# Order of the split products in a half tile of weights: high half first, low half last

## The chip, the cores and the metric

The kernel runs on one core of a Trainium2 chip. The metric is the device time of one execution in microseconds. It is a whole program: weights and activations come from HBM, and the outputs go back to it.

## What is computed

Two passes of one transformer-like layer share their weights: a context pass over 128 tokens and a denoising pass over 128 tokens, each with 2048 features. In short:

```
mod  = silu(c) @ w_ada + b_ada             # six vectors: shift, scale and gate, twice
h    = rmsnorm(x) * (1 + scale1) + shift1
p    = h @ w_in                            # 2048 -> 8192 features
mix  = [gated linear recurrence, short convolution, attention](p)
x    = x + gate1 * (mix @ w_out)           # 2048 -> 2048
h    = rmsnorm(x) * (1 + scale2) + shift2
x    = x + gate2 * ((silu(h @ wg) * (h @ wu)) @ wd)   # hidden width 5632
out  = rmsnorm(x)
```

All of it is in fp32. The weights are read once for both passes, which is nearly all of the 330 MB that the kernel reads.

## The kernel before, in words

**Products in two halves.** [...] To keep the precision, both operands of a large product are split into a high half and the rest: `hi` is the number rounded, `lo` the difference. A product x*w is then the sum of three: x.hi*w.hi, x.lo*w.hi and x.hi*w.lo. The activations lie split already (`lhs[:, s, 0]` and `lhs[:, s, 1]`, `s` being the sample: 0 context, 1 denoising). The weights are split as they come.

**A tile of weights.** A tile is 512 rows by 512 columns, 1 MB, in SBUF as 128 partitions x 4 blocks `k` x 512. `split` (line 238) issues its DMA on SyncE's queue (line 243) into one of four `raw` buffers and splits it in two half tiles of two blocks each: ScalarE copies `hi` from `raw` (line 253), VectorE subtracts to get `lo` (line 254). There are three buffers of each (`HL_BUFS`). For the first two rounds of the input projection the tiles are only half as large, one half tile each.

**The products.** `split_mm` (line 265) goes over the blocks of a tile and over the two samples; for each, `products` (line 258) issues three matmuls of 128x128 by 128x512 into the sample's accumulator `acc[s]` (one accumulator of 512 columns for each sample, two such pairs in all). The order in the source is x.hi*w.hi, x.lo*w.hi, x.hi*w.lo for sample 0, the same for sample 1, and then the next block: twelve matmuls for a half tile, of which eight read `hi` and four `lo`. `last_mm` (line 273) does the last two tiles of an output block in another way: it splits them into buffers of their own, and then runs all products of sample 0 before those of sample 1. `feature_mm` (line 285) is a third form, for narrow tiles with the weights as the stationary operand; its products are at line 304.

**What runs beside it.** The layer's modulation vectors are also products with large weights, `w_ada`. A part of them is done on TensorE between the tiles (`ada_pe`, line 328), on `raw` tiles that are not split. The rest is done on VectorE: `later_dve` (line 397) loads rows of `w_ada` into two buffers `araw` (a small copy on GpSimd at line 407, then a DMA from GpSimd's queue at line 408) and accumulates them with four instructions a piece (line 411). After each tile `behind` (line 442) issues as much of that as the constants `PACE_T` and `PACE_V` allow for the stage.

**The order of the instructions.** The source gives the order only in part. The program is built under a framework (`TileContext` with `schedule_with_timeline_sim=True`, line 1112) that knows what each instruction reads and writes, takes the source's order as a priority and places each engine's instructions by when a model of the chip has their operands ready. `split` stands in a scope of higher priority, in the later stages by 600 (`SPLIT_AHEAD`), so that loads and splits go ahead of other work. Each engine then runs its queue strictly in that order. A `hi` buffer is written again when the last matmul that reads it has ended, and so with `lo`; a `raw` buffer is loaded again when both halves have been made from it.

**The stages.** 0 to 240 us: modulation of the first norm and seven column blocks of the input projection in rounds over the rows; to 525 us: the other column blocks, with recurrence, convolution and attention in between; to 626 us: the output projection; then the second norm and the channel mixer, in two groups of hidden columns.

Of the kernel before, what the change touches and what calls it, by code (L numbers as in the profile page):

```python
# [92 lines left out]
def trunk(ctx: ExitStack, tc: tile.TileContext, a: dict):  # L93
    nc = tc.nc
# [12 lines left out]
    def u4(shape=(P, 2, CH)):  # L107
        return sb(list(shape), "u4", U4_BUFS)

    def u8(shape=(P, 2, 2, 4, P), dt=F32):  # L110
        return sb(list(shape), "u8", U8_BUFS, dt)

    def st(shape=(P, CH), dt=F32):
        return sb(list(shape), "st", ST_BUFS, dt)
# [5 lines left out]
    def accs():  # L120
        r = []
        for s in range(2):
            uid[0] += 1
            r.append(psum.tile([P, CH], F32, tag="acc", name=f"acc_{uid[0]}", bufs=4))
        return r
# [112 lines left out]
    def split(src, apart=False):  # L238

        n = src.shape[1]  # L240
        with tc.high_priority(offset=ahead[0]):
            raw = sb([P, 4, CH], "raw", RAW_BUFS)
            nc.sync.dma_start(raw[:, 0:n], src)
            parts = []
            if apart:
                his, los = u8((P, 4, CH), F32R), u8((P, 4, CH), F32R)
            for j in range(n // 2):
                if apart:
                    hi, lo = his[:, 2 * j:2 * j + 2], los[:, 2 * j:2 * j + 2]
                else:  # L250
                    hi = sb([P, 2, CH], "hi", HL_BUFS, F32R)
                    lo = sb([P, 2, CH], "lo", HL_BUFS, F32R)
                nc.scalar.activation(hi, raw[:, 2 * j:2 * j + 2], AF.Copy)  # L253
                nc.vector.tensor_tensor(lo, raw[:, 2 * j:2 * j + 2], hi.bitcast(F32), op=ALU.subtract)  # L254
                parts.append((hi, lo))
        return parts

    def products(acc, s, k, lhs, lk, parts, first, last):

        hi, lo = parts[k // 2]  # L260
        for i, (x, w) in enumerate(((0, hi), (1, hi), (0, lo))):
            nc.tensor.matmul(acc, lhsT=lhs[:, s, x, lk, :], rhs=w[:, k % 2, :],  # L262
                             start=first and i == 0, stop=last and i == 2)

    def split_mm(src, acc, lhs, first, last, k0=0):

        parts = split(src)
        n = src.shape[1]
        for k in range(n):
            for s in range(2):  # L270
                products(acc[s], s, k, lhs, k0 + k, parts, first and k == 0, last and k == n - 1)

    def last_mm(steps, acc, phase):

        tiles = []
        for src, lhs in steps:
            tiles.append((split(src, True), lhs))
            behind(phase)
        for s in range(2):
            for t, (parts, lhs) in enumerate(tiles):  # L280
                for k in range(4):
                    products(acc[s], s, k, lhs, k, parts, False, t == len(tiles) - 1 and k == 3)
            yield s

    def feature_mm(src, rhs, accs2, first, last):
# [156 lines left out]
    def behind(phase=None):  # L442

        pump()
        if phase is not None:
            ada_step(phase)
# [45 lines left out]
    for nm in ("xp", "xs"):  # L492
        t = u8((P, D))
# [370 lines left out]
    for ri, (k0, nk) in enumerate(ROUNDS):  # L864
        nxt = 4 * ROUNDS[ri + 1][1] // 2 if ri + 1 < len(ROUNDS) else 0
        last = ri == len(ROUNDS) - 1
        if last:
            ahead[0] = SPLIT_AHEAD
        for i, name in enumerate(ORDER[:START]):
            acc = accs()  # L870
            split_mm(w_in(k0 // 4, name)[:, k0 % 4:k0 % 4 + nk, :], acc, hT[k0 // 4], True, True, k0 % 4)
            if ri == 0:
                part[name] = u4()
            for s in range(2):
                if ri == 0:
                    nc.scalar.activation(part[name][:, s, :], acc[s], AF.Copy)
                else:
                    nc.vector.tensor_tensor(part[name][:, s, :], part[name][:, s, :], acc[s], op=ALU.add)  # L878
            behind(0 if last else None)
            if ri == 0 and i == 1:  # L880
                spawn(other_inputs(part[name][:, 0, :]))
            if i < START - 1:
                first_step((nxt * (i + 1)) // (START - 1) - (nxt * i) // (START - 1))
            if last:
                consume(name, part[name])
    for name in ORDER[START:]:
        if name in FM:
            for half in range(2):
                acc = accs()
                for q in range(2):  # L890
                    feature_mm(a["w_infm"][2 * FM.index(name) + half, q],
                               lambda k: tuple(hT[2 * q + k // 4][:, :, x, k % 4, :] for x in range(2)), acc, q == 0, q == 1)
                    behind(1)
                for b in range(2):
                    consume_fm(name, 2 * half + b, acc[b][:, 0:256].rearrange("p (s t) -> p s t", s=2))
            continue
        acc = accs()
        for q in range(4):
            split_mm(w_in(q, name), acc, hT[q], q == 0, q == 3)
            behind(1)  # L900
        t = u4()
        for s in range(2):
            nc.scalar.activation(t[:, s, :], acc[s], AF.Copy)
        consume(name, t)
# [4 lines left out]
    for n in range(4):  # L909
        acc = accs()  # L910
        xr = sb([P, 2, CH], "ld", 2)
        nc.gpsimd.tensor_copy(xr[:, :, 0:1], S["late"][:, :, 0:1])
        for s, nm in enumerate(("xp", "xs")):
            nc.gpsimd.dma_start(xr[:, s, :], a[nm][:, n * CH:(n + 1) * CH])
        if n == 3:
            for p in range(GAP_APART):
                gap[p] = [u4(), u4()]
                for j in range(2):
                    nc.sync.dma_start(gap[p][j], a["w_ada2"][LATER_GAP - 8, p, :, 2 * j:2 * j + 2])

        def add(s):
            t = st()
            nc.vector.tensor_tensor(t, acc[s], g[:, s, :], op=ALU.mult)
            nc.vector.tensor_tensor(x[:, s, :], t, xr[:, s, :], op=ALU.add)
            nc.scalar.activation(t, x[:, s, :], AF.Square, accum_out=ssq2[:, s, n:n + 1])

        many = 4 - LAST_TILES if n == 3 else 4
        for j in range(many):
            split_mm(a["w_out"][n, j], acc, mix[j], j == 0, j == 3)
            behind(2)  # L930
        x = u4()
        x1.append(x)
        g = gate(8 + n)
        for s in last_mm([(a["w_out"][n, j], mix[j]) for j in range(many, 4)], acc, 2):
            add(s)
        if n == 2:
            rest2 = [most(ssq2[:, s, 0:3]) for s in range(2)]
# [57 lines left out]
    for gi, grp in enumerate(groups):  # L995
# [6 lines left out]
        for n in range(4):  # L1002
            acc = accs()
# [7 lines left out]
            for s in last_mm([(a["w_down"][n, grp[j]], fs[j]) for j in range(many, len(grp))], acc, 3):  # L1011
                t = st()
                v = x1[n][:, s, :]
                nc.vector.tensor_tensor(t, acc[s], g[:, s, :], op=ALU.mult)
                nc.vector.tensor_tensor(v, v, t, op=ALU.add)
                if gi == 0:
                    continue
                nc.scalar.activation(t, v, AF.Square, accum_out=ssq3[:, s, n:n + 1])
                if not final:
                    nc.vector.tensor_tensor(v, v, fw[:, n, :], op=ALU.mult)  # L1020
                    if n == 2:
                        rest3.append(most(ssq3[:, s, 0:3]))
                    continue

                r = rms1(ssq3[:, s, 3:4], D, rest3[s])
                out = a["o_ys" if s else "o_yp"]
                for b in (2, 0, 3, 1):
                    v = x1[b][:, s, :]
                    if b == 3:
                        nc.vector.scalar_tensor_tensor(v, v, r, fw[:, 3, :], op0=ALU.mult, op1=ALU.mult)  # L1030
                    elif b == 2:
                        nc.vector.tensor_scalar(v, v, r, None, op0=ALU.mult)
                    else:
                        nc.scalar.activation(v, v, AF.Copy, scale=r)
                    (nc.scalar if b < 2 else nc.sync).dma_start(out[:, b * CH:(b + 1) * CH], v)
# [81 lines left out]
```

## Time and profile before

| | |
|---|---|
| runs | 1393.62 us median of 3 (1393.14 to 1399.99) |
| the profiled execution's own time | 1394.64 us |
| its span, from the first to the last instruction | 1392.8 us |
| mean granted TensorE clock | 0.991 |
| TensorE matmuls, weight loads | 1353.3 us (97%), 1082.0 us (78%) |
| VectorE | 875.9 us (63%) |
| ScalarE | 626.6 us (45%) |
| GpSimd | 135.3 us (10%) |
| matmuls | 7936 |
| HBM read | 330.43 MB, 240 GB/s over the span |

Matmuls overlap one another, so a matmul's own duration (some 0.39 us) is longer than the distance to the next one, and the busy share of TensorE says only that it had a matmul in flight. The distance between starts is its pace. In rows of the trace "L262" is a line of the kernel above, "acc<-hi,u" a matmul that writes `acc` and reads `hi` and a tile of the activations, "x2" two such instructions merged into one row; the time ahead of it is the start of the first, then their joint length. A bracket at the end gives how long the engine was idle before, and what ended that.

### The profile page before, as it was taken

How to read it: one execution, taken by the hardware profiler on the slowest of the kernel's cores; microseconds unless marked ns; L12 is line 12 of the kernel's file. 1: busy time of each engine (PE TensorE's matmuls, PEld its weight loads, DVE VectorE, ACT ScalarE, POOL GpSimd, SP SyncE). 2: the span in 40 equal slices, each digit the busy share in tenths (PEclk: the TensorE clock that was granted, in tenths of full speed). 3: DMA queues.
4: the chain of work that ended last, by engine and by line, in shares of the span. 5: the costliest groups of instructions: out<-in, count | busy, mean ns of one | idle time of the engine just before them, and what ended most of it. 6: DMA issues, size and time to landing. Idle time of an engine off the chain costs nothing.

```text
span 1392.8 us, 19779 instructions
## 1 busy us (share of the span) xinstructions
PE 1353.3 (97%) x7936; PEld 1082.0 (78%) x7936; DVE 875.9 (63%) x1102; ACT 626.6 (45%) x839; POOL 135.3 (10%) x201
## 2 busy tenths in 40 slices
PE   5999999999999999999899999999999999999996
PEld 3666777897798886677788788888888888888885
DVE  3354558987977886467745879545555544455565
ACT  4433347655455443346444344443334344444442
POOL 0100002221222321001200231000000000000000
PEclk9999999999999999999999999999999999999998
DMA  9797887775887988775665667555556555555551
GB/s 345 281 345 276 318 314 271 290 280 206 300 290 263 319 330 319 274 272 190 243 216 182 224 229 273 196 192 185 194 198 215 194 196 181 188 197 190 183 204 67
DMA packets 54380, 335.39 MB, mean 241 GB/s; under 512 B 7248, under 2 KB 7312, under 8 KB 19216
## 3 DMA queue, kind: packets, MB, share of 16 engines
q1 hardware_dynamic: 42768, 296.79, 58.7%
q0 software_dynamic: 10944, 36.29, 7.3%
q8 instruction: 62, 1.02, 0.3%
q10 hardware_dynamic: 576, 1.05, 0.2%
q14 instruction: 30, 0.25, 0.0%
HBM read 330.43 MB, written 3.67 MB: 240 GB/s over the span
## 4 chain that ended last, share of the span: by engine, by line
PE 89%; DMA 5%; issue 3%; DVE 2%; POOL 1%; ACT 1%; SPq 0%; DVEq 0%; POOLq 0%; ACTq 0%
PE acc L262 69%; PE acc L304 10%; PE ada L328 6%; DMA araw<-w_ada 2%; DMA raw<-w_ada 1%; PE aux L452 1%; DMA raw<-w_in 1%; DVE lo L254 1%; POOL araw L407 1%; DMA u<-xp 1%; PE aux L626 0%; PE aux L375 0%; DMA aacc<-b_ada 0%; DVE aacc L411 0%; PE aux L341 0%
## 5 line engine op out<-in xcount | busy, mean ns | idle before, releaser
L262 PE MATMUL acc<-hi,u 128*128 128x512 f32 x2944 | 873.4, 393 | 1.0 <-ACT u L484 0.8
L254 DVE TENSOR_TENSOR lo<-raw,hi 128x1024 fp32r<-128x1024 f32 x368 | 449.2, 1223 | 376.2 <-ACT hi L253 362.3
L262 PEld LDWEIGHTS acc<-hi,u 128*128 128x128 f32 x2944 | 551.6, 189 | 136.8 <-issue 11.2
L253 ACT ACTIVATE hi<-raw 128x1024 fp32r<-128x1024 f32 x368 | 388.7, 1060 | 556.1 <-PE acc L262 471.8
L262 PE MATMUL acc<-lo,u 128*128 128x512 f32 x1472 | 533.1, 394 | 7.1 <-DVE lo L254 7.1
L262 PEld LDWEIGHTS acc<-lo,u 128*128 128x128 f32 x1472 | 274.5, 188 | 77.5 <-DVE lo L254 11.6
L411 DVE SCALAR_TENSOR_TENSOR aacc<-araw,cs,aacc 128x512 f32<-128x512 f32 x224 | 159.4, 746 | 40.7 <-DMA araw<-w_ada 31.1
L304 PE MATMUL acc<-u,hi 128*128 128x256 f32 x768 | 141.8, 286 | 0.0
L304 PEld LDWEIGHTS acc<-u,hi 128*128 128x128 f32 x768 | 119.0, 191 | 7.3 <-issue 5.9
L304 PE MATMUL acc<-u,lo 128*128 128x256 f32 x384 | 108.1, 286 | 0.0
L328 PE MATMUL ada<-raw,cst 128*32 128x256 f32 (+1 forms) x784 | 92.3, 481 | 11.8 <-DMA raw<-w_ada 11.8
L407 POOL COPY araw<-u 128x2 f32<-128x2 f32 x56 | 54.0, 965 | 264.4 <-DVE aacc L411 212.7
L294 ACT ACTIVATE hi<-raw 128x1024 fp32r<-128x1024 f32 x48 | 50.9, 1060 | 64.0 <-PE acc L304 44.0
L304 PEld LDWEIGHTS acc<-u,lo 128*128 128x128 f32 x384 | 72.5, 191 | 5.2 <-issue 2.5
L295 DVE TENSOR_TENSOR lo<-raw,hi 128x1024 fp32r<-128x1024 f32 x48 | 58.4, 1221 | 15.3 <-ACT hi L294 12.5
L328 PEld LDWEIGHTS ada<-raw,cst 128*32 128x32 f32 x784 | 26.4, 113 | 44.3 <-issue 32.1
L878 DVE TENSOR_TENSOR u<-u,acc 128x512 f32<-128x512 f32 x56 | 37.7, 684 | 26.7 <-PE acc L262 26.7
L408 POOL DMA_DIRECT2D araw<-w_ada x56 | 30.0, 536 | 15.5 <-POOL araw L407 15.2
L401 POOL COPY aacc<-u 128x2 f32<-128x2 f32 x7 | 3.8, 536 | 252.3 <-DVE u L878 173.4
L480 ACT ACTIVATE st<-aux,sh,sc 128x128 f32<-128x128 f32 x48 | 18.1, 456 | 14.3 <-DVE sc L349 7.4
L262 PE MATMUL acc<-u,u 128*128 128x512 f32 x96 | 22.1, 389 | 0.0
L262 PEld LDWEIGHTS acc<-u,u 128*128 128x128 f32 x96 | 18.0, 188 | 3.7
(218 smaller groups left out, 631.8 us busy)
## 6 DMA issues: line engine op xcount, KB each, us to landing
raw<-w_ada SPq DMA_DIRECT2D x66, 1024.0 KB, 6.9
raw<-w_gate SPq DMA_DIRECT2D x44, 1024.0 KB, 4.9
raw<-w_up SPq DMA_DIRECT2D x44, 1024.0 KB, 4.8
raw<-w_down SPq DMA_DIRECT2D x44, 1024.0 KB, 4.8
raw<-w_in SPq DMA_DIRECT2D x33, 1024.0 KB, 6.5
araw<-w_ada POOLq DMA_DIRECT2D x56, 512.0 KB, 5.7
raw<-w_infm SPq DMA_DIRECT2D x24, 1024.0 KB, 6.2
raw<-w_out SPq DMA_DIRECT2D x16, 1024.0 KB, 5.8
```

The source lines that it names most:

```text
L253: nc.scalar.activation(hi, raw[:, 2 * j:2 * j + 2], AF.Copy)
L254: nc.vector.tensor_tensor(lo, raw[:, 2 * j:2 * j + 2], hi.bitcast(F32), op=ALU.subtract)
L262: nc.tensor.matmul(acc, lhsT=lhs[:, s, x, lk, :], rhs=w[:, k % 2, :], start=first and i == 0, stop=last and i == 2)
L294: nc.scalar.activation(hi, raw[:, 4 * j:4 * j + 4], AF.Copy)
L295: nc.vector.tensor_tensor(lo, raw[:, 4 * j:4 * j + 4], hi.bitcast(F32), op=ALU.subtract)
L304: nc.tensor.matmul(one, lhsT=w[:, k % 4, ws], rhs=y, start=first and k == 0 and i == 0, stop=last and k == 7 and i == 2)
L328: nc.tensor.matmul(box["acc"][32 * k:32 * k + 32, 0:cols.stop - cols.start], lhsT=cst[:, 4 * part + k, 2 - row:34 - row], rhs=raw[k // 2][ ...
L407: nc.gpsimd.tensor_copy(raw[:, :, 0:1], S["late"][:, :, 0:1])
L408: nc.gpsimd.dma_start(raw, a["w_ada2"][c - 8, part // 2, :, 2 * (part % 2):2 * (part % 2) + 2, :])
L411: nc.vector.scalar_tensor_tensor(acc[:, s, :], raw[:, k, :], cs[:, 2 * part + k, s:s + 1], acc[:, s, :], op0=ALU.mult, op1=ALU.add)
L480: nc.scalar.activation(h[:, s, j, :], ps[:, s, j, :], AF.Identity, bias=bias, scale=scale)
L878: nc.vector.tensor_tensor(part[name][:, s, :], part[name][:, s, :], acc[s], op=ALU.add)
```

## The change

`products` now gets a half tile, that is, two blocks, and the accumulators of one or both samples. It lists all products with `hi` first, for each block and each sample two, and then all with `lo`, and issues them in that order. `split_mm` calls it once for each half tile with both samples, and `last_mm` once for each half tile with one sample. The flags that begin and end a sum go with the first product of each accumulator and with the last. `feature_mm` is as it was.

```diff
-    def products(acc, s, k, lhs, lk, parts, first, last):
-
-        hi, lo = parts[k // 2]
-        for i, (x, w) in enumerate(((0, hi), (1, hi), (0, lo))):
-            nc.tensor.matmul(acc, lhsT=lhs[:, s, x, lk, :], rhs=w[:, k % 2, :],
-                             start=first and i == 0, stop=last and i == 2)
+    def products(accs2, ks, lhs, k0, parts, first, last):
+
+
+
+        hi, lo = parts[ks[0] // 2]
+        todo = [(k, s, acc, x, hi) for k in ks for s, acc in accs2 for x in (0, 1)]
+        todo += [(k, s, acc, 0, lo) for k in ks for s, acc in accs2]
+        n = len(accs2)
+        for i, (k, s, acc, x, w) in enumerate(todo):
+            nc.tensor.matmul(acc, lhsT=lhs[:, s, x, k0 + k, :], rhs=w[:, k % 2, :],
+                             start=first and k == ks[0] and w is hi and x == 0, stop=last and i >= len(todo) - n)
 
     def split_mm(src, acc, lhs, first, last, k0=0):
 
         parts = split(src)
         n = src.shape[1]
-        for k in range(n):
-            for s in range(2):
-                products(acc[s], s, k, lhs, k0 + k, parts, first and k == 0, last and k == n - 1)
+        for k in range(0, n, 2):
+            products([(s, acc[s]) for s in range(2)], (k, k + 1), lhs, k0, parts, first and k == 0, last and k == n - 2)
 
     def last_mm(steps, acc, phase):
 
@@ -278,8 +282,8 @@
             behind(phase)
         for s in range(2):
             for t, (parts, lhs) in enumerate(tiles):
-                for k in range(4):
-                    products(acc[s], s, k, lhs, k, parts, False, t == len(tiles) - 1 and k == 3)
+                for k in (0, 2):
+                    products([(s, acc[s])], (k, k + 1), lhs, 0, parts, False, t == len(tiles) - 1 and k == 2)
             yield s
```

## Rows read from the trace of the kernel before

**Rows 1.** The page, part 1: engine, busy us, share of the span, instructions.

```profile
PE 1353.3 (97%) x7936; PEld 1082.0 (78%) x7936; DVE 875.9 (63%) x1102; ACT 626.6 (45%) x839; POOL 135.3 (10%) x201
```

**Rows 2.** Timeline of a calm half tile: start us, length us, engine, line, instruction.

```profile
955.79 1.06 ACT L253 ACTIVATE hi<-raw 128x1024 fp32r<-128x1024 f32 x1 [1.65 <-PE acc L262]
955.82 1.07 PE L262 MATMUL acc<-hi,u 128*128 128x512 f32 x4
...
956.73 0.62 PE L262 MATMUL acc<-lo,u 128*128 128x512 f32 x2
956.89 1.23 DVE L254 TENSOR_TENSOR lo<-raw,hi 128x1024 fp32r<-128x1024 f32 x1 [0.56 <-ACT hi L253]
...
957.18 0.61 PE L262 MATMUL acc<-hi,u 128*128 128x512 f32 x2
...
957.64 0.39 PE L262 MATMUL acc<-lo,u 128*128 128x512 f32 x1
...
957.86 0.61 PE L262 MATMUL acc<-hi,u 128*128 128x512 f32 x2
...
958.32 0.39 PE L262 MATMUL acc<-lo,u 128*128 128x512 f32 x1
...
958.51 1.06 ACT L253 ACTIVATE hi<-raw 128x1024 fp32r<-128x1024 f32 x1 [1.66 <-PE acc L262]
958.54 1.07 PE L262 MATMUL acc<-hi,u 128*128 128x512 f32 x4
```

**Rows 3.** TensorE's waits: waiting line, releaser, us in total, times, longest us.

```profile
PE ada L328 <- DMA raw<-w_ada: 11.8, 4, 7.1
PE acc L262 <- DVE lo L254: 7.1, 6, 2.3
...
PE acc L262 <- ACT hi L253: 0.2, 1, 0.2
```

**Rows 4.** Busy us by stretch: PE, PEld, DVE, ACT, POOL, PEclk, DMA share, GB/s.

```profile
600.00:700.00 100.00, 94.71 (x458) 75.34 (x457) 75.54 (x123) 46.12 (x69) 12.73 (x22) 0.98 0.65 234
700.00:830.00 130.00, 127.26 (x558) 103.96 (x557) 83.66 (x93) 56.51 (x62) 19.38 (x25) 0.99 0.60 212
...
926.00:1101.00 175.00, 175.00 (x778) 145.05 (x777) 90.69 (x84) 69.89 (x70) 0.72 (x2) 1.00 0.57 199
```

**Rows 5.** Timeline of the first episode, from 669 to 687 us.

```profile
669.02 1.07 PE L262 MATMUL acc<-hi,u 128*128 128x512 f32 x4
669.68 0.75 DVE L411 SCALAR_TENSOR_TENSOR aacc<-araw,cs,aacc 128x512 f32<-128x512 f32 x1 [2.38 <-DMA araw<-w_ada]
...
671.62 0.73 PE L262 MATMUL acc<-lo,u 128*128 128x512 f32 x2 [1.54 <-DVE lo L254]
...
683.20 0.75 DVE L411 SCALAR_TENSOR_TENSOR aacc<-araw,cs,aacc 128x512 f32<-128x512 f32 x1 [3.59 <-DMA araw<-w_ada]
...
685.15 1.22 PE L262 MATMUL acc<-lo,u 128*128 128x512 f32 x2 [2.35 <-DVE lo L254]
...
686.16 1.06 PE L262 MATMUL acc<-hi,u 128*128 128x512 f32 x2
...
687.02 0.63 PE L262 MATMUL acc<-lo,u 128*128 128x512 f32 x1
```

**Rows 6.** Timeline of the second episode, TensorE alone.

```profile
782.71 0.73 PE L262 MATMUL acc<-lo,u 128*128 128x512 f32 x2 [0.41 <-DVE lo L254]
...
796.93 0.73 PE L262 MATMUL acc<-lo,u 128*128 128x512 f32 x2 [2.11 <-DVE lo L254]
```

**Rows 7.** Busy us around the two long waits, columns as in rows 4.

```profile
670.00:685.00 15.00, 11.26 (x49) 8.93 (x48) 11.41 (x14) 6.55 (x8) 3.02 (x4) 1.00 0.64 233
685.00:688.50 3.50, 3.35 (x8) 2.71 (x9) 3.50 (x6) 0.00 (x0) 1.12 (x1) 0.51 0.67 207
...
797.70:801.10 3.40, 3.40 (x9) 2.65 (x8) 3.40 (x5) 1.06 (x1) 1.03 (x1) 0.50 0.86 306
```

**Rows 8.** VectorE's waits: waiting line, releaser, us in total, times, longest us.

```profile
DVE aacc L411 <- DMA araw<-w_ada: 31.1, 18, 3.9
```

## Prediction

> **What bounds the kernel now.** I read the page's busy times first, then TensorE's waits, the busy time by stretch, and at last the timeline of single half tiles. TensorE's matmuls are busy 97% of the span [rows 1]. A busy share can hide slow matmuls, so the pace comes from the timeline of an undisturbed half tile [rows 2]. Its twelve products start at 955.82 and the next half tile's at 958.54: 2.72 us for twelve, 0.227 us for one, and no gap among them. So from end to end the kernel runs at TensorE's pace, and an edit that only reorders products can win no more than TensorE's idle time. The list of its waits says how much of that belongs to this edit [rows 3]: 7.1 us in 6 waits for `lo`, 0.2 us for `hi`. The longest entry, 11.8 us for the first weights of w_ada, has no product of the changed lines in it.
>
> By stretch, the idle time that isn't the start or the end of the kernel stands between 600 and 830 us: 5.3 us of 100 and 2.7 us of 130, while from 926 to 1101 us TensorE is busy without a break [rows 4]. Only there can the change give anything back.
>
> The same half tile shows that the order on the chip isn't the order of the source [rows 2]. The source asks for hi, hi, lo, then hi, hi, lo; the trace has four hi, two lo, two hi, one lo, two hi, one lo. Whatever orders the instructions already holds the first lo product back from third place to fifth. That is the main reason why I expect little.
>
> **The change, part by part.**
>
> *Products.* Nothing is added or removed: twelve products and twelve weight loads per half tile before and after, so 0.227 us each and 0 us of work gained or lost. What the edit could change in the price of a product is the number of times that consecutive products go to the other sample's accumulator: by the observed order 6 per half tile, by the new one 8. The two lo products at 956.73, one for each sample, take 0.45 us to the next start (957.18), and the two hi products of one sample at 957.18 take 0.46 (957.64) [rows 2]. A price of a change below 0.005 us cannot be excluded, which over 2 more changes in 368 half tiles is under 3.7 us; I take 0, since the pair with the change is no slower.
>
> The Trainium skill, page "TensorE: Matmul & The Clock Gate", section "A second HAM failure mode: psum-queue depth-cycling", speaks against this edit: a kernel that cycled through accumulator banks from one iteration to the next idled briefly between groups of matmuls and had its clock switched down and up. By that rule more alternation could cost clock; by the rows above the alternation that there already is costs none. It is a rival below.
>
> *When lo is needed.* The first lo product moves from fifth to ninth place: 4 x 0.227 = 0.91 us later, in every half tile.
>
> *When hi comes free.* The last hi product moves from eleventh to eighth place, so ScalarE, which starts the next `hi` when that product has ended (958.51, after a wait of 1.66 us) [rows 2], can start 3 x 0.227 = 0.68 us earlier, and VectorE's `lo`, which in the calm stretch starts 0.04 us after its `hi`, follows. The buffer of `lo` comes free after the twelfth product as before. So where VectorE is not behind, `lo` gains 0.68 us of lead on top. There the lead is ample already: with three buffers the `lo` that ends at 956.89 + 1.23 = 958.12 belongs to the half tile that starts two periods after 955.82, at 961.26, and its first product comes 0.91 later, at 962.17: a lead of 4.05 us. So in the calm stretches both edits are worth 0 us; the lead covers them, and without it the price would be a wait of TensorE in each half tile.
>
> *The stalls.* In the first episode TensorE has issued the four hi products at 669.02, wants lo at 669.93 and gets it at 671.62, a wait of 1.54 us by the row; at 685.15 it waits 2.35 us [rows 5]. Both times VectorE had stood still (2.38 and 3.59 us) in front of an accumulation of w_ada rows whose DMA had not landed, and `lo` was queued behind that accumulation. So `lo` was late because of a DMA, not for want of `hi`; the earlier `hi` cannot help and the 0.91 us can. It helps once: if the first wait shrinks by 0.91, TensorE reaches the second one 0.91 earlier but needs that lo 0.91 later, and so waits there as long as before, since VectorE works through its queue between the two without ever waiting for TensorE. The second episode is the same: 0.41 us at 782.71, 2.11 us at 796.93 [rows 6]; again 0.91 in all. Two small waits make up the rest of the 7.1. So the term is 2 x 0.91 = 1.8 us, with 0.3 us for the small ones: 2.1 us. From below it is 0, if the lo moves back in VectorE's queue as far as it moves in TensorE's; from above it is all 7.1 us.
>
> *The clock.* After the wait at 685.15 the granted clock over 3.5 us was 0.51, which is the lower level, 1.2 GHz, for nearly all of it [rows 7]; two products (686.16 to 687.02) take 0.86 us in place of 0.45 [rows 5], 0.2 us more for each, and 8 of them 1.6 us. After 796.93 the clock was at 0.50 for another 3.4 us [rows 7], the same price again. What TensorE did before was wait 2.35 and 2.11 us; after the wait of 1.54 us the clock stayed at 1.00, up to 685 us [rows 7]. I leave both drops in place, as the long wait of each episode shrinks little: 0 us; the upper bound is 2 x 1.6 = 3.2 us.
>
> *Evictions.* The first sample's sum is complete at the eleventh place of the last half tile and not at the ninth, 0.45 us later, the second sample's as before. TensorE has another pair of accumulators to fill for at least a half tile, 2.72 us, meanwhile, so 0 us; without that cover it would be 0.45 us for each pair. In the last step of an output block the two samples are run one after the other, and the end of each is where it was.
>
> **Sum.** 1394.64 us is the profiled execution's own time (1392.8 of span, 1.8 around it). Minus 2.1 is 1392.5. The median of the runs is 1.0 us lower than the profiled one, so I predict 1391.5 us, 0.15% faster. A difference under 0.5%, 7 us, is about what a measurement of this kernel cannot tell from none.
>
> **The rivals.** *All stalls go.* For it: the lead grows by 0.91 + 0.68 = 1.6 us, and the order of VectorE's queue is chosen anew; if the lo comes ahead of the accumulations there, no DMA can hold it. Then 7.1 us of waits and 3.2 us of low clock vanish: 1393.6 - 10.3 = 1383.3 us. Against it: VectorE's waits for those rows are up to 3.9 us long [rows 8], and in both episodes it had fallen behind before.
>
> *The lo falls back in VectorE's queue.* This one ends slower. A product that is wanted 0.91 us later may be prepared later: with a new order one more accumulation may stand in front of each lo. VectorE waits 18 times for those DMA, 31.1 us together [rows 8], and at present 7.1 us of waiting for lo reach TensorE. The place is VectorE's queue, wherever w_ada rows are accumulated; the point from which it decides is a lead used up, some 4 to 5 us of delay in a row. If a third of the other 24 us came through, it would be 8 us: 1401.6 us. Against it: `lo` is still issued ahead of the time, and the extra 0.91 us has to be used up first.
>
> *Nothing changes.* The trace's order already has lo fifth; if the new order on the chip again differs from the source's and lo stays where it was, the time stays at 1393.6 us.
>
> *Alternation costs clock.* If more changes of accumulator made TensorE pause, it would show in each half tile; at the bound of 0.005 us it is 1397.3 us, and clock drops on top, each at 1.6 us, would take it over 1401 with three. The rows speak against it. By the skill's section named above this one would be likelier than I make it.
>
> **How the numbers follow.** Chances: the forecast, one shift per episode, 0.45; all or nearly all stalls gone 0.25; lo falls back 0.17; nothing changes 0.10; alternation 0.03. Faster than 1386.6 needs most of the 10.3 us: the second case and a little of the first, 0.28. Slower than 1400.6: the third case for the most part and a little of the last, 0.17. The rest, 0.55, is within 0.5%. The range goes from 1383, where all stalls are gone, to 1400, which takes in the alternation's bound and the milder half of the third case; the rest of that case and what might lie beyond 1383 are the 2 in 10 left out.
>
> **What would show it.** Right: eight hi products and then four lo in the rows of a half tile; a pace of 0.227 us; ScalarE's `hi` starting after the eighth product; waits for `lo` down to between 4 and 6 us, still behind accumulations that waited for their DMA; one or two stretches of lower clock at those places. Wrong: no waits for `lo` at all (then the new order of VectorE's queue did more than the order of products), waits of 10 us and more in places that have none now, or a pace other than 0.227 us in the stretch from 926 to 1101 us.

## The result and the profile after

The changed kernel takes 1379.01 us (median of 4 runs, 1374.68 to 1380.55), the kernel before 1393.71 us on the same chip (1393.14 to 1399.99). The ratio is 0.9882, interval 0.9864 to 0.9901: 14.7 us or 1.2% faster, outside the predicted range. The profiled execution is the fastest of the four, 1374.68 us with a span of 1372.9 us, so the two profiles differ by 19.9 us of span. The profile of the experiment e1 below, at 1379.60 us, stands near the median; where the two differ, both are told.

The page of the changed kernel, busy time by engine, answers to [rows 1]:

```profile
PE 1338.6 (97%) x7936; PEld 1078.0 (79%) x7936; DVE 872.9 (64%) x1102; ACT 627.4 (46%) x839; POOL 132.6 (10%) x201
```

The share is 97% as before and the count of matmuls is the same, yet TensorE is busy 14.7 us less. Three quarters of what the profiles differ by was busy time, which the prediction had held to be work that must be done.

The order and the pace are as forecast. A calm half tile after, to be held against [rows 2]:

```profile
930.28 1.98 PE L267 MATMUL acc<-hi,u 128*128 128x512 f32 x8
...
932.09 1.07 PE L267 MATMUL acc<-lo,u 128*128 128x512 f32 x4
932.29 1.06 ACT L253 ACTIVATE hi<-raw 128x1024 fp32r<-128x1024 f32 x1 [1.66 <-PE acc L267]
...
933.00 0.39 PE L267 MATMUL acc<-hi,u 128*128 128x512 f32 x1
```

Eight products with `hi`, four with `lo`, 933.00 - 930.28 = 2.72 us for twelve, and ScalarE's next `hi` starts when the eighth has ended. The stretch from 926 to 1101 us is as busy as it was, and the two stretches ahead of it, with 5.3 and 2.7 us idle before [rows 4], have 2.6 and nothing left, at full clock:

```profile
600.00:700.00 100.00, 97.36 (x476) 78.11 (x475) 75.18 (x119) 49.13 (x71) 12.76 (x19) 1.00 0.65 236
700.00:830.00 130.00, 130.00 (x587) 107.84 (x586) 90.62 (x101) 57.64 (x63) 21.91 (x28) 1.00 0.61 219
926.00:1101.00 175.00, 175.00 (x778) 145.05 (x777) 90.12 (x85) 70.94 (x70) 0.72 (x2) 1.00 0.56 198
```

TensorE's waits, as in [rows 3]:

```profile
PE ada L332 <- DMA raw<-w_ada: 11.3, 4, 7.2
...
PE acc L267 <- DVE lo L254: 1.7, 3, 0.7
...
PE acc L267 <- ACT hi L253: 0.8, 1, 0.8
```

The waits for `lo` went from 7.1 us to 1.7 us. VectorE does not stand less in front of its late DMA, but more (31.1 us before [rows 8]):

```profile
DVE aacc L415 <- DMA araw<-w_ada: 38.8, 24, 5.5
```

The longest of them shows why little of it arrives at TensorE:

```profile
644.05 2.08 DVE L415 SCALAR_TENSOR_TENSOR aacc<-araw,cs,aacc 128x512 f32<-128x512 f32 x3 [5.48 <-DMA araw<-w_ada]
...
645.12 1.97 PE L267 MATMUL acc<-hi,u 128*128 128x512 f32 x8
646.05 1.22 DVE L254 TENSOR_TENSOR lo<-raw,hi 128x1024 fp32r<-128x1024 f32 x1
...
647.32 0.96 PE L267 MATMUL acc<-lo,u 128*128 128x512 f32 x3 [0.23 <-DVE lo L254]
```

VectorE stood for 5.48 us, and its `lo` is finished only at 646.05 + 1.22 = 647.27 us. TensorE has eight `hi` products to run from 645.12 on and loses 0.23 us. With the old order it would have wanted `lo` after four of them, at 645.12 + 4 x 0.227 = 646.03 us, and by this estimate waited 1.3 us.

The largest single part lies in rows that the prediction never opened: the products with `w_ada`, which are on no line of the diff. Busy time of these alone by stretch, first before, then after (columns: us, PE busy and matmuls, PEclk, DMA share, GB/s):

```profile
0.00:240.00 240.00, 50.79 (x544) 0.98 0.82 309
240.00:525.00 285.00, 28.26 (x176) 1.00 0.79 285
525.00:700.00 175.00, 15.23 (x80) 0.99 0.71 257
```

```profile
0.00:240.00 240.00, 46.80 (x544) 0.99 0.83 311
240.00:525.00 285.00, 28.64 (x176) 1.00 0.78 287
525.00:700.00 175.00, 10.03 (x80) 1.00 0.74 271
```

The same 800 matmuls take 4.0 us less in the first stretch and 5.2 us less in the last. A half tile in which this happens looks so, before and then after:

```profile
107.47 1.07 PE L262 MATMUL acc<-hi,u 128*128 128x512 f32 x4
108.47 1.06 PE L328 MATMUL ada<-raw,cst 128*32 128x256 f32 x10
109.46 0.73 PE L262 MATMUL acc<-lo,u 128*128 128x512 f32 x2
```

```profile
103.12 1.09 PE L332 MATMUL ada<-raw,cst 128*32 128x256 f32 x16
104.14 1.21 PE L267 MATMUL acc<-hi,u 128*128 128x512 f32 x4
```

A tile of `w_ada` gives 16 such products, four for each 32 columns of the array. Before, ten of them stand between four `hi` and the first `lo`, and from their start to the next product it is 0.99 us. After, all sixteen stand together between two half tiles and take 1.02 us. So ten cost what sixteen cost, and a tile that is cut in two can be paid for twice. That whole packs cost so little agrees with the Trainium skill, page "TensorE: Matmul & The Clock Gate", section "Part 3: Packing small matmuls — row/col tiling": matmuls on different parts of the array run at the same time. The section does not speak of a pack that is cut.

A block is from here on an unbroken run of `w_ada` products in TensorE's order. The trace of before has 81 of them, 17 of these between a `hi` and a `lo` of `split_mm`; the trace after has 73, and 3. To account for a whole span I took, for each matmul, the time from its start to the next one's start, less the time with none in flight, and summed by kind. The idle time is what lies between the first and the last matmul. "Excess" is what the products of 512 columns with the main weights take beyond 0.2267 us each: low clock, and the changes to and from other products. Low clock is what the trace has of it between 50 us and the last 20 us.

| profile | span | `w_ada` blocks | `w_ada` us | excess us | all else us | idle us | low clock us |
|---|---|---|---|---|---|---|---|
| before | 1392.8 | 81 | 88.5 | 25.4 | 216.5 | 21.6 | 10.2 |
| after | 1372.9 | 73 | 80.3 | 18.6 | 216.6 | 16.2 | 0 |
| e1 | 1377.8 | 73 | 80.2 | 19.8 | 216.9 | 20.0 | 3.4 |
| e2 | 1393.8 | 81 | 88.4 | 24.3 | 216.3 | 24.0 | 3.4 |
| e3 | 1390.3 | 76 | 86.0 | 20.7 | 216.5 | 25.9 | 6.8 |
| e4 | 1379.7 | 73 | 81.1 | 20.1 | 218.5 | 19.2 | 10.2 |
| e8 | 1380.8 | 73 | 80.9 | 17.0 | 219.3 | 22.7 | 6.8 |
| e9 | 1394.4 | 77 | 87.0 | 21.3 | 216.8 | 28.4 | 13.7 |
| e6 | 1379.6 | 67 | 73.9 | 21.0 | 219.6 | 21.7 | 10.2 |
| e7 | 1374.5 | 67 | 75.2 | 17.5 | 219.4 | 18.8 | 10.2 |
| e12 | 1388.5 | 69 | 75.3 | 21.2 | 222.6 | 25.6 | 20.5 |
| e11 | 1375.2 | 68 | 74.3 | 17.3 | 218.5 | 21.8 | 6.8 |
| e10 | 1390.3 | 84 | 92.5 | 21.1 | 216.8 | 19.0 | 6.8 |
| e13 | 1422.0 | 116 | 104.6 | 24.9 | 221.4 | 27.4 | 6.8 |

From before to after: the blocks take 8.2 us less, the excess 6.8 and idle time 5.4, together 20.4 us against 19.9 of span. From before to e1, the profile near the median: 8.3, 5.6 and 1.6 us less and 0.4 more in the rest, together 15.1 against 15.0. So the 8 us of the blocks are in both, and what the waits and the clock give back differs between executions. Of the excess, a stretch of low clock is worth 1.6 us (the prediction's own price); there are three before (at 60.4, 685 and 798 us), one in e1, none after, which makes 3.2 or 4.8 us. The other 2 or so are the fewer changes to and from a block: outside low clock, a product right ahead of a block or right behind one takes 0.10 us more than the pace, and there are 107 of these before and 82 after, which makes 2.6 us.

### The profile page after: what moved, and what is told of

The parts are those of the page before. It is cut to its first block, busy times and chain, and to the rows that moved or that the text cites. A ratio compares the mean times of both kernels' runs of the same rounds, so it can differ in the third digit from the quotient of the medians.

```text
span 1372.9 us, 19781 instructions
## 1 busy us (share of the span) xinstructions
PE 1338.6 (97%) x7936; PEld 1078.0 (79%) x7936; DVE 872.9 (64%) x1102; ACT 627.4 (46%) x839; POOL 132.6 (10%) x201
## 3 DMA queue, kind: packets, MB, share of 16 engines
q8 instruction: 62, 1.02, 0.3%
## 5 line engine op out<-in xcount | busy, mean ns | idle before, releaser
L267 PE MATMUL acc<-hi,u 128*128 128x512 f32 x2944 | 741.2, 393 | 2.0 <-ACT u L488 1.1
L267 PE MATMUL acc<-lo,u 128*128 128x512 f32 x1472 | 397.1, 390 | 1.8 <-DVE lo L254 1.7
L332 PE MATMUL ada<-raw,cst 128*32 128x256 f32 (+1 forms) x784 | 83.7, 484 | 11.3 <-DMA raw<-w_ada 11.3
L882 DVE TENSOR_TENSOR u<-u,acc 128x512 f32<-128x512 f32 x56 | 35.9, 682 | 25.0 <-PE acc L267 24.9
```

Of the source, the lines that this page charges most:

```text
L267: nc.tensor.matmul(acc, lhsT=lhs[:, s, x, k0 + k, :], rhs=w[:, k % 2, :], start=first and k == ks[0] and w is hi and x == 0, stop=last and ...
L332: nc.tensor.matmul(box["acc"][32 * k:32 * k + 32, 0:cols.stop - cols.start], lhsT=cst[:, 4 * part + k, 2 - row:34 - row], rhs=raw[k // 2][ ...
```

## The experiments

Each ratio sets the median of an experiment against that of the kernel before, which ran beside each group of kernels: at 1395.40 us beside e1 to e4, 1396.01 beside e6 to e9 and 1393.64 beside e10 to e13. The interval behind a ratio is the 95% interval.

**Which of the two callers?** e1 has the new order in `split_mm` alone (`last_mm` calls the old function, here under another name), e2 in `last_mm` alone.

```diff
-                for k in (0, 2):
-                    products([(s, acc[s])], (k, k + 1), lhs, 0, parts, False, t == len(tiles) - 1 and k == 2)
+                for k in range(4):
+                    products1(acc[s], s, k, lhs, k, parts, False, t == len(tiles) - 1 and k == 3)
```

> Hi first, lo last in split_mm alone; last_mm in the old order. Lead (lo needed four places later, hi free three places earlier): all of the gain stays, 1379 us within 3, waits of TensorE for lo under 3 us. Cuts (the unsplit w_ada products, which the old order let into the middle of half tiles, are cut into fewer blocks, each cut costing up to 1 us): the same 1379 us, 72 blocks of w_ada products where before has 79 or 80. New plan (any change of order gives another plan, and the plan before was an unlucky one): anything from 1372 to 1395 us.

> Hi first, lo last in last_mm alone; split_mm in the old order. Lead: no gain, 1393 us within 2, waits for lo of about 7 us. Cuts: no gain either, 79 or 80 blocks. New plan: anything from 1375 to 1395 us.

e1: 1380.32 us, ratio 0.9896 (0.9863 to 0.9929). e2: 1396.13 us, 1.0003 (0.9988 to 1.0018). All of the gain comes from `split_mm`. TensorE's waits for `lo`, e1 and then e2, and in e1 the stretch after its longest wait (busy time by engine, PEclk behind them):

```profile
PE acc L267 <- DVE lo L254: 4.5, 3, 2.3
```

```profile
PE acc L274 <- DVE lo L254: 7.3, 6, 2.1
```

```profile
669.30:672.70 3.40, 3.06 (x7) 2.48 (x8) 3.40 (x6) 3.00 (x4) 1.06 (x1) 0.51 0.49 182
```

e1 still waits 4.5 us and falls to the lower clock once, just what the prediction had forecast for the changed kernel; and yet it is 15 us faster than before. So the waits for `lo`, 2.6 us less than before, are only a small part of the gain.

**Later `lo`, or earlier `hi`?** The edit does both. e3 puts the `lo` products behind the `hi` products of each block, so that the first `lo` is fifth as in the trace of before. e4 is the changed kernel with the last `hi` product moved to the very end, so that `lo` is late but `hi` comes free later than before.

```diff
-        todo = [(k, s, acc, x, hi) for k in ks for s, acc in accs2 for x in (0, 1)]
-        todo += [(k, s, acc, 0, lo) for k in ks for s, acc in accs2]
+        todo = []
+        for k in ks:
+            todo += [(k, s, acc, x, hi) for s, acc in accs2 for x in (0, 1)]
+            todo += [(k, s, acc, 0, lo) for s, acc in accs2]
```

```diff
+        todo = todo[:4 * len(accs2) - 1] + todo[4 * len(accs2):] + [todo[4 * len(accs2) - 1]]
```

> For each of the two blocks of a half tile four hi products and then two lo. The first lo stands fifth in nearly every half tile, as it did in most of them in the kernel before, and hi is free after the tenth product. Lead: waits for lo of 5 to 7 us and one or two stretches of low clock, so little gain from them; with 73 blocks of w_ada products in place of 79, cuts give 6 us: 1387 us. Lead alone: 1391 us. New plan: anything from 1372 to 1395 us.

> Seven hi products, the four lo, and one hi last: lo is needed in eighth place, but hi is free only after the twelfth. If the later need of lo gives the gain: waits for lo under 3 us, 1379 to 1382 us. If the earlier release of hi gives it: waits for lo of 5 us and more, and 1385 to 1390 us. Cuts alone (72 blocks): 7 us of gain in any case, 1387 us.

e3: 1388.39 us, 0.9957 (0.9941 to 0.9973). e4: 1382.10 us, 0.9899 (0.9875 to 0.9924). The waits for `lo`, e3 and then e4:

```profile
PE acc L269 <- DVE lo L254: 7.0, 7, 2.0
```

```profile
PE acc L268 <- DVE lo L254: 3.4, 2, 1.8
```

With `lo` fifth the sum of the waits is that of before; with `lo` late and `hi` held to the end nearly all of the gain is there (13 us, where e1 in the same group has 15). So most of the gain goes with the later place of `lo`, and the earlier release of `hi` is worth at most the 2 to 3 us between e4 and the changed kernel. That e3 still gains 0.4% belongs to the other part: its blocks, 76 against 81, take 2.5 us less and its excess is 4.7 us smaller, one stretch of low clock among it, while its idle time is longer.

The waits of e3 do not stand where those of before stood, and that separates two causes. The stretches of [rows 4] in e3:

```profile
600.00:700.00 100.00, 94.73 (x461) 75.93 (x460) 75.61 (x123) 46.45 (x70) 16.66 (x23) 0.98 0.65 231
700.00:830.00 130.00, 130.00 (x587) 107.82 (x586) 85.60 (x92) 58.65 (x66) 18.39 (x24) 1.00 0.64 226
```

Around the first episode e3 is as idle as before: its waits for `lo` between 658 and 686 us are 4.4 us together, where before has 3.9. In the second episode, where before waits 2.8 us between 783 and 810 us and falls to the lower clock, e3 is busy without a break, although its `lo` is fifth; it has 2.7 us of waits between 852 and 872 us instead. What e3 shares with the changed kernel there is the order of VectorE's instructions: 171 accumulations stand ahead of the `lo` that starts at 776 us before, 161 ahead of the same `lo` in e3 and in the changed kernel. At the `lo` of the first episode the three differ by three at most. So the end of the second episode goes with VectorE's new order, and not with the place of `lo` in TensorE's. The changed kernel, e1, e4 and e8 have no wait for `lo` between 780 and 812 us either, while e2, whose VectorE runs its accumulations and `lo` in exactly the order of before, waits 2.4 us there.

**Alternation.** e8 is the changed kernel with the accumulator changed after every product, 11 times within a half tile and once more to the next; so counted, the changed kernel has 7 and one more, the 8 of the prediction.

```diff
-        todo = [(k, s, acc, x, hi) for k in ks for s, acc in accs2 for x in (0, 1)]
+        todo = [(k, s, acc, x, hi) for k in ks for x in (0, 1) for s, acc in accs2]
```

> The changed kernel, but the eight hi products alternate between the two samples' accumulators at each step: eleven changes of accumulator in a half tile in place of seven, and lo needed and hi freed at the same places. Lead and cuts: as the changed kernel, 1379 us within 3, 0.227 us for a product. If alternation has a price: slower than the changed kernel, by 1.5 us for each nanosecond. New plan: up to 10 us to either side, since the plan may differ.

1380.72 us, 0.9888 (0.9862 to 0.9915), the same as the changed kernel. Its calm half tile, starts and lengths:

```profile
930.00 1.98 PE L267 MATMUL acc<-hi,u 128*128 128x512 f32 x8
931.82 1.07 PE L267 MATMUL acc<-lo,u 128*128 128x512 f32 x4
932.72 1.98 PE L267 MATMUL acc<-hi,u 128*128 128x512 f32 x8
```

932.72 - 930.00 = 2.72 us, the same pace. Changing the accumulator has no price here.

**Are VectorE's late accumulations what makes `lo` late?** e9 is the kernel before with the rows of `w_ada` for VectorE loaded once for each of the two buffers and used again after that: GpSimd's copy and 54 of the loads are left out, so the sums are of the same rows over and over, and no accumulation waits for a DMA.

```diff
-        raw = sb([P, 2, CH], "araw", 2)
-        nc.gpsimd.tensor_copy(raw[:, :, 0:1], S["late"][:, :, 0:1])
-        nc.gpsimd.dma_start(raw, a["w_ada2"][c - 8, part // 2, :, 2 * (part % 2):2 * (part % 2) + 2, :])
+        if ("araw", part % 2) not in S:
+            S["araw", part % 2] = const([P, 2, CH], f"araw{part % 2}")
+            nc.gpsimd.dma_start(S["araw", part % 2], a["w_ada2"][c - 8, part // 2, :, 2 * (part % 2):2 * (part % 2) + 2, :])
+        raw = S["araw", part % 2]
```

> The kernel before, but VectorE's accumulations use two pieces of w_ada rows loaded once; the other 54 loads, and the copies of GpSimd ahead of them, are left out, so those modulation gates are not the reference's. If lo was late because of accumulations that waited for their DMA: no waits for lo above 0.5 us from 600 to 830 us and no low clock there, 7 to 10 us gone, with 75 blocks of w_ada products another 2 to 4: 1381 to 1387 us. If lo was late for another reason: waits for lo stay at 5 us and more, and 1390 us.

1397.52 us, 1.0009 (0.9996 to 1.0023): no gain, where one was expected. TensorE's waits:

```profile
PE aux L470 <- DVE u L954: 10.3, 1, 10.3
...
PE acc L262 <- DVE lo L254: 0.5, 1, 0.5
```

The waits for `lo` are gone, 0.5 us of the 7.1, as the theory of the late DMA says. But the second norm now keeps TensorE waiting for 10.3 us in one piece, with 10.2 us of low clock at 634 us. VectorE's instructions stand in another order once the accumulations no longer depend on a DMA: from 631.58 to 641.52 us eleven of them stand among the norm's small steps, where before has none, and what was saved is lost there. So the run shows the mechanism, and not its worth.

**Blocks kept whole.** e6 (on the kernel before) and e7 (on the changed one) give the `w_ada` products a higher priority, so that once a tile has arrived all its products go in one piece. No product is added, removed or changed.

```diff
-        for k in range(4):
+        with tc.high_priority(offset=600):
+            for k in range(4):
...
```

> The kernel before, with the w_ada products on TensorE in a scope of higher priority (600), so that none of their blocks is cut by products of the split tiles: 66 blocks in place of 79, and the order of the split products as before. Cuts: 8 fewer blocks went with 8 us in the changed kernel, so 13 fewer give 8 to 13 us here: 1382 to 1387 us, with TensorE's time on w_ada products down from 97 to about 85 us and the waits for lo at about 7 us. Lead alone: no gain, 1393 to 1395 us. New plan: anything from 1372 to 1400 us.

> The changed kernel with the same scope of priority for the w_ada products: 66 blocks in place of 72. Cuts: 4 to 6 us less than the changed kernel, 1373 to 1376 us, w_ada products at about 84 us. Lead alone: no gain over the changed kernel, 1379 us. New plan: anything from 1370 to 1395 us.

e6: 1387.66 us, 0.9939 (0.9917 to 0.9961); its profile is of its fastest run, 1381.39 us. e7: 1376.40 us, 0.9852 (0.9820 to 0.9883). Both have 67 blocks, and the blocks take 73.9 and 75.2 us against 88.5 and 80.3. The priority alone, on the old order, brings 8.4 us. It goes with a later start (e6):

```profile
PE ada L329 <- DVE r_t L206: 9.6, 1, 9.6
...
PE acc L262 <- DVE lo L254: 4.4, 3, 2.1
```

The first matmul starts at 9.6 us, before at 7.1.

**The same, with the start left alone.** e11 (changed kernel) and e12 (kernel before) raise the priority only after the first of the modulation's vectors.

```diff
+        whole[0] = 600 if v > 0 else 0
...
-        for k in range(4):
+        with tc.high_priority(offset=whole[0]):
+            for k in range(4):
...
```

> The changed kernel with the higher priority for the w_ada products from the second group of columns on, so that the start is as it was: 66 blocks in place of 72. Cuts: the 2.6 us that the run with the priority from the first group on lost at its start stay, so 1373 to 1375 us, w_ada products busy for about 80 us. Lead alone: 1379 us.

> The same priority in the kernel before: 66 blocks in place of 79, the old order of the split products. Cuts: 12 to 15 us less on w_ada products, less what new waits take, 1381 to 1386 us; waits for lo as in the kernel before. The rest to the changed kernel with the same priority, 8 to 11 us, is the lead's share.

e11: 1375.43 us, 0.9875 (0.9857 to 0.9894). e12: 1387.85 us, 0.9956 (0.9934 to 0.9978), above what was expected. The start did not come back, so it is not the offset of 600 on the first products that delays it; why it is late stays open. e11's first wait, and then e12's:

```profile
PE ada L334 <- DVE r_t L207: 9.5, 1, 9.5
```

```profile
PE ada L330 <- DMA raw<-w_ada: 20.0, 8, 10.1
...
PE acc L263 <- DVE lo L255: 3.3, 4, 2.2
```

The blocks of e12 are as cheap as e11's (75.3 and 74.3 us). Of the 20.0 us that e12 waits for weights of `w_ada`, 10.1 are its start; the other 9.9 are to be held against 11.8 - 7.1 = 4.7 before [rows 3] and 7.2 in e11. e12 has six stretches of low clock, e11 two. At equal blocks the order of the products is thus worth 12.4 us by the medians of e12 and e11, and 11.3 by those of e6 and e7. With the blocks cut as they were it is 14.7. The gains do not add: where blocks are whole already, the order has little of them left to save. In the two profiles, 13.3 us apart, the blocks make 1.0, idle time 3.8, the excess 3.9 and the rest 4.1 us. Why the old order loses more there by waits and clock is not shown: only one of e12's six stretches of low clock follows a wait for a `lo` of `split_mm` (2.20 us, at 792 us).

**More cuts.** e10 is the changed kernel with the part of the `w_ada` products that is queued behind the tiles (`later_pe`) cut on purpose: each call does one half of a tile, four products and not eight.

```diff
+        part, half = divmod(part, 2)
...
-        e = ada_pe(a["w_ada2"][c - 8, part], box, part, [(ALL, 2 if kind == 4 else 0)], first, last)
+        e = ada_pe(a["w_ada2"][c - 8, part], box, part, [(ALL, 2 if kind == 4 else 0)], first, last,
+                   range(2 * half, 2 * half + 2))
```

e13 raises the priority of the `w_ada` products only for the later stages (`whole[0] = 600` set ahead of the loop over the later column blocks, 0 until then). In the first stage, where the offset is 0, the products came out in many more blocks, which makes it a run on cuts.

> The changed kernel with the later w_ada products on TensorE issued in halves, one half at a time: 83 blocks of them in place of 72, the same products in all and the split products in the same order. Cuts: a half block of 512 columns takes as long as a whole one, 0.98 us, so 11 more blocks give 11 us: 1388 to 1391 us, and TensorE's busy time on w_ada products rises from 86 to 95 us or more. Lead alone: no change, 1379 us. New plan: up to 10 us to either side.

> The changed kernel in a plan that cuts the early w_ada products in many pieces: 115 blocks in place of 72, most of the new ones single products of 256 columns for each of two pieces, in the first 240 us. Cuts: a block of two of those took 0.55 us in the kernel before, so 43 more blocks give some 24 us: 1400 to 1406 us. Lead alone: 1379 us.

e10: 1391.61 us, 0.9980 (0.9965 to 0.9996), 12.6 us above the changed kernel with 11 more blocks; the kernel before ran at nearly the same time beside both (1393.64 and 1393.71). e13: 1422.34 us, 1.0204 (1.0176 to 1.0232), 43.3 us above it with 43 more. The `w_ada` products by stretch in e10 (columns as above), and single blocks of e13:

```profile
240.00:525.00 285.00, 37.78 (x170) 1.00 0.76 275
```

```profile
36.04 1.09 PE L334 MATMUL ada<-raw,cst 128*32 128x256 f32 x16
37.06 1.21 PE L268 MATMUL acc<-hi,u 128*128 128x512 f32 x4
...
41.40 0.62 PE L334 MATMUL ada<-raw,cst 128*32 128x256 f32 x2
41.95 1.20 PE L268 MATMUL acc<-hi,u 128*128 128x512 f32 x4
...
43.54 1.08 PE L334 MATMUL ada<-raw,cst 128*32 128x256 f32 x14
44.55 2.11 PE L268 MATMUL acc<-hi,u 128*128 128x512 f32 x8
```

Sixteen products of 256 columns: 1.02 us. Two and fourteen: 0.55 and 1.01, together 1.56. In e10 the blocks cost 12.2 us more than in the changed kernel for 11 (92.5 against 80.3), all in the stretch where the cut was made (37.78 us against 28.64) and the next. Against e1, whose profile is as near its median as e10's, the blocks make 12.3 of 12.5 us of span. e13 was expected at 0.55 us a block and came out at twice that. The blocks themselves do cost 0.57 each (24.3 us for 43), but the changes to and from them take another 6.3 us, the narrow products and the rest 4.8, and 11.2 us are new idle time, with 2.6 more ahead of the first matmul: 49.2 us, as the two profiles' spans differ (1422.0 and 1372.9). So the kernel lost more than the blocks took. Not all of that is the cuts': a wait of TensorE for the second norm, 3.2 to 3.3 us, stands in each of the five kernels whose priority is raised there (e6, e7, e11, e12, e13). The rest of the idle time was not taken apart.

## Why the prediction was wrong

**The step that failed** is in its first paragraph: "So from end to end the kernel runs at TensorE's pace, and an edit that only reorders products can win no more than TensorE's idle time." The pace was read from a calm half tile at 955 us, where it is right, and carried to stretches where TensorE also runs the `w_ada` blocks. There a busy TensorE is not doing a fixed amount of work: what the blocks cost depends on how many pieces they are in, and the new order of the products changed that, from 81 to 73. It was followed by "Nothing is added or removed ... so ... 0 us of work gained or lost", which holds for the twelve products and not for what is put between them. The entry of 11.8 us in [rows 3] was set aside with the words that it "has no product of the changed lines in it"; that wait stayed, at 11.3 us, but the group that it belongs to became 8.2 us cheaper. A look at the `w_ada` group's own rows before predicting, its 17 blocks between a `hi` and a `lo` at 1 us each for the most part, would have bounded the term: joining them to others could save at most the 17.2 us that they take together.

Why they stood there is not shown. One reading is that where the order is made and `lo` isn't ready for its first product, the next ready products are those of `w_ada`, and they go in as far as the hole reaches; with `lo` last there are 3 such blocks for 17. But e4, where `lo` comes late too, has 12 of them, more than the 8 of e3, and still 73 blocks at 81.1 us; so the number between a `hi` and a `lo` alone does not decide it. What is shown is that the four kernels with `lo` late (the changed one, e1, e4, e8) have 73 blocks each and the others 81 (before, e2) and 76 (e3), which speaks against a plan that was better by chance. What cuts cost is shown by e10 and e6, where the order of the products within a half tile stays the same; e13, where the idle time has another part too, agrees.

**The clock** was left as it was ("I leave both drops in place"). Its price was right, its place not: both drops are gone in the profiled execution, and so is one at 60.4 us that the prediction did not count; in e1 one is left. At that price the term is 3.2 to 4.8 us where 0 was taken and 3.2 was the upper bound.

**The waits for lo**: 2.1 us were forecast to go, 5.4 went in the profile, and 2.6 in e1's. The mechanism, one VectorE queue in which `lo` stands behind accumulations with a late DMA, was right (e9, and the rows at 644 us). But that e1 comes near the 2.1 us is luck: by "It helps once" each episode was to give 0.91 us, and in e1 the first one is as long as before (1.69 + 2.26 us against 1.54 + 2.35) while the second is gone, as in e3, where VectorE's order is new too. In the first episode the waits of the kernels with `lo` late run from 1.7 us (the changed kernel) to e1's 3.95, and runs of the kernel before spread over 9 us too (1390.5 to 1399.8).

**Right**: the order on the chip and the pace of 0.227 us; `hi` released earlier being worth little (e4); nothing from `last_mm`'s evictions (e2); alternation free (e8). The Trainium skill, page "TensorE: Matmul & The Clock Gate", section "A second HAM failure mode: psum-queue depth-cycling", tells of a kernel whose clock went up and down while it cycled through accumulator banks. e8 does not show it: with 11 changes in each half tile the pace stayed at 2.72 us, and the granted clock from 926 to 1101 us at 1.00.

**The rivals.** "All stalls go" came nearest with 1383.3: its waits and clock, 10.3 us, are about what the profiled execution shows for both (5.4 + 4.8), but it had no term for the blocks. The second episode's end goes with a new order of VectorE's queue, on which this rival rested. The `lo` that falls back in VectorE's queue didn't occur: from about 765 to 875 us up to 14 fewer accumulations stand ahead of a `lo` than before, and from 655 to 695 us at most three fewer or one more. How much of the shorter waits in the first episode is due to the later place was not separated from what varies between executions.

## What to carry to other kernels

Before saying that a reordering can win only idle time, list what else the busy engine runs between the lines that the edit touches, and count in how many pieces it runs it: small matmuls that run side by side on parts of the array cost by the piece here, and a piece of two could cost what a piece of eight did. An operand that is ready late was best used last; that a scheduler fills the hole ahead of it with whatever is ready, and cuts that to fit, is a reading that was not tested. A new order on one engine brings a new order on the others, so compare their queues as well before a gain is put down to the edited lines. Keeping such pieces whole by priority is worth trying by itself: the fastest kernels here have both (e7 and e11, 1376.40 and 1375.43 us, where the change alone has 1379.01, though their intervals overlap).

## What was not expected of the hardware

Products of 512 columns on a quarter of the array take 0.98 us for a block of two of them and 1.00 us for a block of eight (means of 7 and of 20 blocks before); at 256 columns it is 0.55 us for two, 0.98 for four and 1.0 for sixteen. In these blocks the number of columns and how many products share one quarter set the time, and not how many quarters are used. And the length of a single wait did not tell whether the lower clock followed. In e1 it followed a wait of 2.26 us and not one of 1.69:

```profile
664.36 1.19 PE L267 MATMUL acc<-lo,u 128*128 128x512 f32 x4 [1.69 <-DVE lo L254]
...
669.64 2.07 PE L267 MATMUL acc<-lo,u 128*128 128x512 f32 x4 [2.26 <-DVE lo L254]
```

But in e4 3.4 us at 0.50 followed a wait of 1.84 us (at 671.20 us), and in e13 a wait of 3.28 us left the clock at 1.00 from 650 to 700 us:

```profile
665.50 1.60 PE L475 MATMUL aux<-u,u 128*128 128x128 f32 x12 [3.28 <-DVE u L960]
```

```profile
650.00:700.00 50.00, 44.57 (x233) 35.63 (x226) 30.07 (x63) 22.96 (x41) 8.18 (x9) 1.00 0.37 132
```
